# A hybrid decoder trunk: the attention's exponentials turned by VectorE and GpSimd transfers, and the mixers' small transfers taken off the weight queue

## The chip, the cores and the metric

The kernel runs on one core of one Trainium2 chip. The core has TensorE (PE), VectorE (DVE), ScalarE (ACT), GpSimd (POOL) and SyncE (SP); each takes its instructions in the order of the program. SP issues DMA transfers, and so can ACT and POOL. The metric is the device time of one execution in microseconds, as the median of several runs.

## The reference

Two layers of a decoder trunk for one sequence of 256 positions and a model width of 2048, all in float32:

```
for l in range(2):
    h = rms_norm(x, mix_norm[l])
    h = mixer_ab(h, ...) if l == 0 else mixer_c(h, ...)
    x = x + h
    x = x + conv_ffn(rms_norm(x, ffn_norm[l]), ...)     # gated, hidden width 5632
```

`mixer_ab` has one input projection whose parts go to two mixers: a chunked spatial gating (parts u and v) and HGRN2, a gated linear recurrence over 8 heads (q, f, i, g). `mixer_c` is attention with 16 heads of width 128, swept in blocks of 128 queries:

```
q, k, v, g, f = split(h @ w_in)
q = rms_norm(q per head, q_gain);  k = rms_norm(k per head, k_gain)
c = cumsum(log_sigmoid(f + b_f))                        # per head
s = q k^T * 128**-0.5 + c[query] - c[key]               # causal
o = softmax(s) @ v                                      # per head and query block
return (o * sigmoid(g)) @ w_out
```

For a head there are three blocks of 128 x 128 scores: queries 0-127 with keys 0-127, and queries 128-255 with keys 0-127 and 128-255.

## The kernel before, in words

**Weights.** All matrices are streamed once from HBM, 820 pieces of mostly 128 x 1024 values. SP's queue loads a piece into `w` (four buffers), ACT rounds it to `wh` (L175), DVE takes the rest `wl = w - wh` (L176), and PE multiplies in three parts: high by high, high by low, low by high (L292 to L294 in `project_tok`, L311 to L313 in `project_four`). One piece is 12 matmuls of 512 columns. `wh` and `wl` have three buffers here, so that ACT and DVE run some pieces ahead of PE.

**Turning a result.** `project_four` and `project_tok` leave tokens on the partitions, and most consumers want features there. So the result is evicted to `z`, DVE turns its 32 x 32 blocks into `tmp` (`blocks`, L324), and 16 small transfers of 32 KB put the blocks in place (`moves`, L331, rows of 256 bytes). Before the change these 16 alternate between SP's queue, where the weight loads are, and POOL's. This is done for f (`gates`), u (`spatial`), the gated HGRN output (`gated`), q and k of the attention, its gate (`gate`), and the results of both output projections (`add_four`), and for the FFN (`zt`), which the change leaves as it is.

**Order.** Side work is written as generators. `tick()` runs once ahead of each weight piece and takes every generator in flight to its next `yield`; `depth[0]` says how many may be in flight. A generator that has started transfers yields `LAG` = 6 times before it reads what they bring. `held` ties an instruction behind the latest `wh` or `wl`. The order on each engine is then set by the framework's scheduler, from these ties and from its own estimates; it is fixed when the kernel is built.

**Attention.** `mixer_c` handles four groups of four heads. For a group it projects q, k and v, and queues one generator `attend` per head, two in flight. In `attend`: ACT copies q and k with their gains (`qk`, L949); after one yield PE makes the scores (L954, L955), DVE adds the biases `ct` and `cb` and the causal mask and takes the maxima (L958 to L968), ACT takes the exponentials in place with their sums (`sc`, L98), DVE the reciprocals (L972). Two yields later PE turns the three blocks (L977) into PSUM, ACT copies them to `pt` (L980), and one yield later PE multiplies with v (L984 to L986) and ACT scales the result into `o` (L988). `cb` is spread over the partitions by a store to DRAM and four loads on POOL's queue (L928, L934). Then come the gate projections (`w_cg`), with `gate` waiting until all heads are done, and the output projections (`w_co`).

Of the kernel before, what the change touches and what calls it, by code (L numbers as in the profile page):

```python
# [15 lines left out]
P = 128  # L16
S = 256
# [8 lines left out]
LAG = 6  # L26
FORGET = 4
WAIT = 4
PACE = 4
# [24 lines left out]
def tile_trunk(ctx: ExitStack, tc: tile.TileContext, x, pp_d, cst_d, mlev_d, msk_d,  # L54
# [261 lines left out]

    def transposed(src, tmp, dst, queues=(nc.sync, nc.gpsimd)):

        blocks(src, tmp)
        moves(tmp, dst, queues)  # L320
# [5 lines left out]

    def moves(tmp, dst, queues=(nc.sync, nc.gpsimd), rows=range(4)):
        n = 2 * BLK
        for a in rows:
            for b in range(4):  # L330
                queues[(a + b) % len(queues)].dma_start(dst[BLK * b:BLK * (b + 1), :, a * n:(a + 1) * n],  # L331
                                  tmp[BLK * a:BLK * (a + 1), b * 4 * n:(b + 1) * 4 * n]
                                  .rearrange("p (m r) -> p m r", m=4))
# [125 lines left out]

    def add_four(q, ps, z, tmp, dst, nxt, halves=1):  # L460
        for T in range(2):
            SC.activation(z[:, T], ps[T], AF.Copy)
        blocks(lambda T: z[:, T], tmp)
        moves(tmp, dst, rows=range(4 // halves))

        def rest():
            if halves == 2:
                yield
                moves(tmp, dst, rows=range(2, 4))
            for _ in range(LAG - 2 * (q == 3)):  # L470
                yield
            for i in range(4):
                m = 4 * q + i
                held(V.tensor_tensor(xT[m], xT[m], dst[:, i], ALU.add), "wl")
                nxt.feed(m)
                if q < 3 or i % 2:
                    yield
            if q == 3:
                for _ in range(WAIT):
                    yield  # L480
                yield from nxt.finish_tok()

        queue.append(rest())


    def mixer_ab(norm):
# [281 lines left out]
        def gated(j):  # L768
# [42 lines left out]
        def spatial(j, z):  # L811
            for _ in range(LAG):
                yield
# [9 lines left out]
        for j in range(2):  # L823
# [4 lines left out]
            t = hp.tile([P, 1024], F32, tag="tok", name=nm("turn"), bufs=2)  # L828
            transposed(lambda T: z[:, T * 512:(T + 1) * 512], tmp, t.rearrange("p (m t) -> p m t", m=4))
            depth[0] = 4  # L830
# [14 lines left out]
        for q in range(4):  # L845
# [12 lines left out]
            if q == 0:  # L858
                depth[0] = 2
            add_four(q, ps, z, tmp, dst, nxt, 2 if q in (1, 2) else 1)  # L860
        es.close()
# [4 lines left out]
    def mixer_c(norm):  # L866
# [21 lines left out]
        R, Rt = norm.finish(), norm.Rt  # L888
        yB = []
        gq = hp.tile([P, LANE], F32, tag="gq", name="gq")[:, 0:1]  # L890
# [53 lines left out]

        def attend(h, q, k, v, o):
            d0 = (h % 4) * P
            qk = hp.tile([P, 2, S], F32, tag="qk", name=nm("qk"), bufs=2)
            for j, (t, g) in enumerate(((q, gq), (k, pp[:, C_KN:C_KN + 1]))):
                r = SC.activation(qk[:, j].rearrange("p (t n) -> p t n", t=2), turned(t[:, h % 4]), AF.Copy, scale=g)  # L949
                if j == 0:  # L950
                    held(r)
            yield
            sp = bank()
            PE.matmul(sp[:, 0:P], qk[:, 0, 0:P], qk[:, 1, 0:P], start=True, stop=True)  # L954
            PE.matmul(sp[:, P:3 * P], qk[:, 0, P:S], qk[:, 1], start=True, stop=True)  # L955
            sc = hp.tile([P, 3, P], F32, tag="sc", name=nm("sc"), bufs=3)
            scf = sc.rearrange("p a b -> p (a b)")
            V.scalar_tensor_tensor(scf[:, 0:P], sp[:, 0:P], ct[:, 0, h:h + 1], cb[:, h, 0:P],  # L958
                                   ALU.add, ALU.subtract)
            V.scalar_tensor_tensor(scf[:, P:3 * P], sp[:, P:3 * P], ct[:, 1, h:h + 1], cb[:, h],  # L960
                                   ALU.add, ALU.subtract)
            V.tensor_tensor(sc[:, 0::2], sc[:, 0::2], cst[:, K_CM:K_CM + P].unsqueeze(1)
                            .to_broadcast([P, 2, P]), ALU.add)
            mxs = hp.tile([P, LANE], F32, tag="mxs", name=nm("mxs"), bufs=2)[:, 0:2]
            sms = hp.tile([P, LANE], F32, tag="sms", name=nm("sms"), bufs=4)[:, 0:2]
            parts = ((0, P), (P, 3 * P))
            for T, (a, b) in enumerate(parts):
                V.tensor_reduce(mxs[:, T:T + 1], scf[:, a:b], AX.X, ALU.max, negate=True)  # L968
            for T, (a, b) in enumerate(parts):
                last = act(scf[:, a:b], scf[:, a:b], AF.Exp, bias=mxs[:, T:T + 1],  # L970
                           accum_out=sms[:, T:T + 1])
            V.reciprocal(sms, sms)  # L972
            yield
            yield
            pps = bank()
            for b in range(3):
                r = PE.transpose(pps[:, b * P:(b + 1) * P], sc[:, b], ident)  # L977
                tc.add_manual_dep(r.ins, last.ins.name, order, reason="in a row")
            pt = hp.tile([P, 3 * P], F32, tag="pt", name=nm("pt"), bufs=2)
            SC.activation(pt, pps[:, 0:3 * P], AF.Copy)  # L980
            yield
            op = bank()
            v0, v1 = (v[:, T, d0:d0 + P] for T in range(2))
            PE.matmul(op[:, 0:P], pt[:, 0:P], v0, start=True, stop=True)  # L984
            PE.matmul(op[:, P:S], pt[:, P:S], v0, start=True, stop=False)
            PE.matmul(op[:, P:S], pt[:, S:3 * P], v1, start=False, stop=True)  # L986
            for T in range(2):
                SC.activation(o[:, T, d0:d0 + P], op[:, T * P:(T + 1) * P], AF.Copy, scale=sms[:, T:T + 1])  # L988
            left[0] -= 1

# [9 lines left out]
        for g in range(CH // 4):  # L1000
            qkv = []
            ss = hp.tile([P, 2, 2, LANE // 4], F32, tag="ss", name=nm("ss"), bufs=2)[..., 0:4]
            for j in range(3):
# [12 lines left out]
                if j < 2:  # L1016
# [11 lines left out]
            os_.append(piece("o", CH // 4))  # L1028
            queue.extend(attend(h, *qkv, os_[g]) for h in range(4 * g, 4 * g + 4))

        room = []

        def gate(q, z):
# [7 lines left out]
            for _ in range(2 * (q < 2)):  # L1041
                yield
            moves(tmp, heads(t))
            for _ in range(LAG - 2 * (q == 3)):
                yield
            for i in range(4):
                if not room:
                    tag, n = ("big", 8) if not yB else ("o", 2)
# [4 lines left out]
                yB.append(y)  # L1053
                yield

        for q in range(CH // 4):
# [4 lines left out]
            queue.append(gate(q, z))  # L1061
        nxt = Norm(C_FFN + KT, turn=True)
        for q in range(4):
            ps = project_four(w_co[4 * q:4 * q + 4], yB, KT)
            add_four(q, ps, piece("z", 2), flat(piece("tmp", 2)), heads(piece("turn", 4)), nxt)
# [4 lines left out]
    def ffn(l, norm, last):  # L1070
# [69 lines left out]
        def add_y(q, finish):  # L1140
            tmp, zt = room()
            near = last and q == 2
            transposed(lambda T: y[:, T, q * 512:(q + 1) * 512], tmp, zt,
                       (nc.sync, nc.gpsimd, SC) if near else (nc.sync, nc.gpsimd))

# [155 lines left out]
```

## Time and profile before

| what | value |
|---|---|
| median of three runs | 2288.69 us (2287.63, 2288.69, 2288.85) |
| profiled execution, its span (the page gives no other time for it) | 2287.3 us |
| busy: PE, DVE, ACT, POOL | 2280.8, 1559.8, 1309.6, 361.2 us |
| granted TensorE clock (1.000 is full speed) | 1.000 |
| DMA | 480.45 MB, mean 210 GB/s; busy 5 to 8 tenths in each slice |

Stages by the span's clock: mixer A and B up to about 390 us, the first FFN to about 1100, the attention to about 1410, its gate and output projections to about 1585, the second FFN to the end. In the groups of the profile a line stands with its engine, operation and tiles, the busy time and the mean duration in ns, and then the idle time ahead of it with what ended that. A busy time is the union of the group's instructions; matmuls overlap, so a matmul's duration is not what it costs the stream. In the chain, SPq is the issuing side of SP's queue.

### The profile page before, as it was taken

To read this page: it belongs to the slowest core of one execution; us is meant where nothing else is said; L and a number is where in the kernel's file an instruction comes from. 1 tells how busy PE (TensorE), PEld (TensorE's weight loads), DVE (VectorE), ACT (ScalarE), POOL (GpSimd) and SP (SyncE) were. 2 spreads that over 40 slices of the span, in tenths; PEclk is the share of its full clock that TensorE was granted. 3 is DMA by queue.
4 is the path that set the end of the run, shared out by engine and by line. 5 is a ranking of instruction groups with operands and counts; after the bars stand their busy time and mean duration, and the time that the engine had idled before them with its cause. 6 is when DMAs were issued, how large, how long until landed. Compare 5 with 4: busy or idle time off the path is not lost.

```text
span 2287.3 us, 32261 instructions
## 1 busy us (share of the span) xinstructions
PE 2280.8 (100%) x10832; PEld 1893.5 (83%) x10832; DVE 1559.8 (68%) x2309; ACT 1309.6 (57%) x1980; POOL 361.2 (16%) x662
## 2 busy tenths in 40 slices
PE   9999999999999999999999999999999999999999
PEld 8888888888888888888888888888888888888887
DVE  7788767777467656766875675767776476657766
ACT  7677756666456445654565555655665465456642
POOL 0121221212012002111111111211211012012102
PEclk9999999999999999999999999999999999999999
DMA  8655767778667667776666655777777677667765
GB/s 288 195 169 160 215 199 235 238 216 234 193 208 221 206 201 213 220 213 186 213 227 203 194 177 181 220 224 242 225 217 218 195 216 210 209 205 216 223 204 174
DMA packets 489415, 480.45 MB, mean 210 GB/s; under 512 B 114112, under 2 KB 457168, under 8 KB 489120
## 3 DMA queue, kind: packets, MB, share of 16 engines
q1 hardware_dynamic: 467040, 453.54, 64.2%
q0 software_dynamic: 20480, 22.50, 4.3%
q10 hardware_dynamic: 1728, 2.35, 0.3%
q8 instruction: 85, 1.39, 0.3%
q14 instruction: 82, 0.67, 0.1%
HBM read 435.24 MB, written 2.11 MB: 191 GB/s over the span
## 4 chain that ended last, share of the span: by engine, by line
PE 97%; DVE 2%; ACT 1%; issue 0%; SPq 0%; DMA 0%; DVEq 0%; ACTq 0%
PE pm L311 26%; PE pm L312 26%; PE pm L313 26%; PE pm L292 4%; PE pm L294 4%; PE pm L293 4%; PE pm L193 1%; PE pm L266 1%; PE pm L217 1%; DVE wl L176 0%; PE pm L269 0%; ACT wh L175 0%; DVE kq L701 0%; PE px L955 0%; SPq L331 0%
## 5 line engine op out<-in xcount | busy, mean ns | idle before, releaser
L176 DVE TENSOR_TENSOR wl<-w,wh 128x1024 fp32r<-128x1024 f32 (+1 forms) x820 | 996.9, 1219 | 637.0 <-ACT wh L175 629.3
L175 ACT ACTIVATE wh<-w 128x1024 fp32r<-128x1024 f32 (+1 forms) x820 | 862.5, 1054 | 786.0 <-PE pm L313 552.3
L311 PE MATMUL pm<-wh,a 128*128 128x512 f32 x1728 | 674.4, 390 | 0.0
L312 PE MATMUL pm<-wl,a 128*128 128x512 f32 x1728 | 672.5, 389 | 0.0
L313 PE MATMUL pm<-wh,a 128*128 128x512 f32 x1728 | 672.5, 389 | 0.0
L331 POOL DMA_DIRECT2D zt<-tmp x413 | 223.5, 549 | 1201.6 <-DVE tmp L324 1089.8
L313 PEld LDWEIGHTS pm<-wh,a 128*128 128x128 f32 x1728 | 324.4, 188 | 67.4
L312 PEld LDWEIGHTS pm<-wl,a 128*128 128x128 f32 x1728 | 324.4, 188 | 67.3 <-DVE wl L176 0.5
L311 PEld LDWEIGHTS pm<-wh,a 128*128 128x128 f32 x1728 | 324.4, 188 | 67.1
L311 PE MATMUL pm<-wh,hid 128*128 128x512 f32 x688 | 267.6, 389 | 0.0
L312 PE MATMUL pm<-wl,hid 128*128 128x512 f32 x688 | 267.6, 389 | 0.0
L313 PE MATMUL pm<-wh,hid 128*128 128x512 f32 x688 | 267.6, 389 | 0.0
L331 POOL DMA_DIRECT2D turn<-tmp x160 | 86.7, 550 | 504.5 <-DVE tmp L324 256.7
L292 PE MATMUL pm<-wh,a 128*128 128x512 f32 x416 | 165.2, 397 | 0.0
L294 PE MATMUL pm<-wh,a 128*128 128x512 f32 x416 | 162.1, 390 | 0.0
L293 PE MATMUL pm<-wl,a 128*128 128x512 f32 x416 | 162.0, 389 | 0.0
L311 PEld LDWEIGHTS pm<-wh,hid 128*128 128x128 f32 x688 | 129.2, 188 | 26.9
L313 PEld LDWEIGHTS pm<-wh,hid 128*128 128x128 f32 x688 | 129.2, 188 | 26.8
L312 PEld LDWEIGHTS pm<-wl,hid 128*128 128x128 f32 x688 | 129.2, 188 | 26.7
L1105 ACT ACTIVATE conv<-zt,pp 128x256 f32<-128x256 f32 x176 | 95.9, 589 | 26.1 <-DMA zt<-tmp 22.2
L324 DVE STREAM_TRANSPOSE tmp<-z 128x512 f32<-128x512 f32 x120 | 83.4, 704 | 18.9 <-ACT z L1091 18.4
L294 PEld LDWEIGHTS pm<-wh,a 128*128 128x128 f32 x416 | 78.1, 188 | 16.6
(244 smaller groups left out, 2075.6 us busy)
## 6 DMA issues: line engine op xcount, KB each, us to landing
w<-in_w_up SPq DMA_DIRECT2D x352, 512.0 KB, 4.4
w<-in_w_dn SPq DMA_DIRECT2D x176, 512.0 KB, 4.5
w<-in_w_cqkv SPq DMA_DIRECT2D x96, 512.0 KB, 4.3
w<-in_w_abo SPq DMA_DIRECT2D x32, 512.0 KB, 4.6
w<-in_w_cg SPq DMA_DIRECT2D x32, 512.0 KB, 4.3
w<-in_w_co SPq DMA_DIRECT2D x32, 512.0 KB, 4.3
zt<-tmp SPq DMA_DIRECT2D x414, 32.0 KB, 2.7
zt<-tmp POOLq DMA_DIRECT2D x413, 32.0 KB, 2.5
```

The source lines that it names most:

```text
L175: r = deep["wh"] = SC.activation(wh, w, AF.Copy)
L176: deep["wl"] = V.tensor_tensor(wl, w, wh.bitcast(F32), ALU.subtract)
L193: PE.matmul(ps[g][T], a[:, o + T * P:o + (T + 1) * P], t[:, i * 512:(i + 1) * 512], start=k + i + j == 0, stop=k + i == KT - 1 and j == 2)
L292: PE.matmul(ps[T], ah, h, start=k + i == 0, stop=False)
L293: PE.matmul(ps[T], ah, l, start=False, stop=False)
L294: deep["last"] = PE.matmul(ps[T], al, h, start=False, stop=k + i == KT - 1)
L311: PE.matmul(ps[T], ah, h, start=not begun and k + i == ks[0], stop=False)
L312: PE.matmul(ps[T], ah, l, start=False, stop=False)
L313: deep["mm"] = deep["last"] = PE.matmul(ps[T], al, h, start=False, stop=not more and k + i == ks[-1] + 1)
L324: V.transpose(tmp.rearrange("p (b m i t) -> p b m i t", b=4, m=4, t=2)[:, :, :, :, T], src(T).rearrange("p (m b j) -> p b m j", m=4, b=4))
L331: queues[(a + b) % len(queues)].dma_start(dst[BLK * b:BLK * (b + 1), :, a * n:(a + 1) * n], tmp[BLK * a:BLK * (a + 1), b * 4 * n:(b + 1) * ...
L1105: held(SC.activation(c, z, AF.Identity, bias=pp[:, cb:cb + 1], scale=w(2)))
```

## The change

In the attention PE no longer turns the exponentials. `attend` takes two heads, their scores share one buffer of six blocks; DVE turns the 32 x 32 blocks of the exponentials into `ptmp`, and 16 transfers on POOL's queue, in rows of 128 bytes, build `pt` for both heads. The value matmuls follow `LAG - 1` yields after the last transfers. A pair starts at least `PAIR` = 5 ticks after the one before it.

All small transfers of the mixers go on POOL's queue alone, except where `q` is 3 in `gate` and `add_four`. Those that read them wait one more yield. The two halves of `add_four` for the second and third results are gone. The depth is 3 while the gate is projected, and `yB` is filled by index.

```
+PAIR = 5
+    ONE, TWO = (nc.gpsimd,), (nc.sync, nc.gpsimd)
-    def moves(tmp, dst, queues=(nc.sync, nc.gpsimd), rows=range(4)):
+    def moves(tmp, dst, queues=TWO):
...
-    def add_four(q, ps, z, tmp, dst, nxt, halves=1):
+    def add_four(q, ps, z, tmp, dst, nxt):
...
-        moves(tmp, dst, rows=range(4 // halves))
+        moves(tmp, dst, ONE if q < 3 else TWO)
         def rest():
-            if halves == 2:
-                yield
-                moves(tmp, dst, rows=range(2, 4))
-            for _ in range(LAG - 2 * (q == 3)):
+            for _ in range(LAG + 1 - 3 * (q == 3)):
                 yield
...
         def gates(j, z):
-            for _ in range(LAG):
+            for _ in range(LAG + 1):
...
-            transposed(lambda T: z[:, T * 512:(T + 1) * 512], tmp, t.rearrange("p (m t) -> p m t", m=4))
+            transposed(lambda T: z[:, T * 512:(T + 1) * 512], tmp, t.rearrange("p (m t) -> p m t", m=4), ONE)
...
-            moves(tmp, t.rearrange("p (m t) -> p m t", m=4))
-            for _ in range(LAG - 1):
+            moves(tmp, t.rearrange("p (m t) -> p m t", m=4), ONE)
+            for _ in range(LAG):
...
-        def attend(h, q, k, v, o):
+        turn = [0]
+        def attend(hs, q, k, v, o):
+            while steps[0] < turn[0]:
+                yield
+            turn[0] = steps[0] + PAIR
...
-            sc = hp.tile([P, 3, P], F32, tag="sc", name=nm("sc"), bufs=3)
+            sc = hp.tile([P, 6, P], F32, tag="sc", name=nm("sc"), bufs=1)
...
             yield
             yield
-            pps = bank()
-            for b in range(3):
-                r = PE.transpose(pps[:, b * P:(b + 1) * P], sc[:, b], ident)
-                tc.add_manual_dep(r.ins, last.ins.name, order, reason="in a row")
-            pt = hp.tile([P, 3 * P], F32, tag="pt", name=nm("pt"), bufs=2)
-            SC.activation(pt, pps[:, 0:3 * P], AF.Copy)
-            yield
+            tmp = hp.tile([P, 6 * P], F32, tag="ptmp", name=nm("ptmp"), bufs=1)
+            for i, sms in enumerate(sums):
+                V.reciprocal(sms, sms)
+                t = V.transpose(tmp.rearrange("p (b m i) -> p b m i", b=4, m=6)[:, :, 3 * i:3 * i + 3],
+                                sc[:, 3 * i:3 * i + 3].rearrange("p m (b j) -> p b m j", b=4))
+                if i == 0:
+                    held(t, "wl")
+            yield
+            n = 6 * BLK
+            pt = hp.tile([P, 6, P], F32, tag="pt", name=nm("pt"), bufs=2)
+            for a in range(4):
+                for b in range(4):
+                    nc.gpsimd.dma_start(pt[BLK * b:BLK * (b + 1), :, BLK * a:BLK * (a + 1)],
+                                        tmp[BLK * a:BLK * (a + 1), b * n:(b + 1) * n]
+                                        .rearrange("p (m r) -> p m r", m=6))
+                if a == 1:
+                    yield
+            for _ in range(LAG - 1):
+                yield
...
-                    transposed(lambda T: z[:, T], flat(piece("tmp", 2)), heads(t))
+                    transposed(lambda T: z[:, T], flat(piece("tmp", 2)), heads(t), ONE)
...
-            moves(tmp, heads(t))
-            for _ in range(LAG - 2 * (q == 3)):
+            moves(tmp, heads(t), ONE if q < 3 else TWO)
+            for _ in range(LAG + 1 - 3 * (q == 3)):
```

`spatial` changes as `gates` does.

More of the change, by code (lines that the diff above doesn't have):

```diff
@@ L315, in project_four, with transposed @@
         return ps
-    def transposed(src, tmp, dst, queues=(nc.sync, nc.gpsimd)):
+    ONE, TWO = (nc.gpsimd,), (nc.sync, nc.gpsimd)
+    def transposed(src, tmp, dst, queues=TWO):
         blocks(src, tmp)
@@ L811, in spatial @@
         def spatial(j, z):
-            for _ in range(LAG):
+            for _ in range(LAG + 1):
                 yield
@@ L859, in mixer_ab @@
                 depth[0] = 2
-            add_four(q, ps, z, tmp, dst, nxt, 2 if q in (1, 2) else 1)
+            add_four(q, ps, z, tmp, dst, nxt)
         es.close()
@@ L960, in attend @@
[L960 to L972, printed above, removed]
+            sps = []
+            for qk in qks:
+                sp = bank()
+                PE.matmul(sp[:, 0:P], qk[:, 0, 0:P], qk[:, 1, 0:P], start=True, stop=True)
+                PE.matmul(sp[:, P:3 * P], qk[:, 0, P:S], qk[:, 1], start=True, stop=True)
+                sps.append(sp)
@@ new lines, in attend @@
+            sums = []
+            for i, (h, sp) in enumerate(zip(hs, sps)):
+                c0 = 3 * P * i
+                parts = ((c0, c0 + P), (c0 + P, c0 + 3 * P))
+                V.scalar_tensor_tensor(scf[:, c0:c0 + P], sp[:, 0:P], ct[:, 0, h:h + 1], cb[:, h, 0:P],
+                                       ALU.add, ALU.subtract)
+                V.scalar_tensor_tensor(scf[:, c0 + P:c0 + 3 * P], sp[:, P:3 * P], ct[:, 1, h:h + 1], cb[:, h],
+                                       ALU.add, ALU.subtract)
+                V.tensor_tensor(sc[:, 3 * i:3 * i + 3:2], sc[:, 3 * i:3 * i + 3:2],
+                                cst[:, K_CM:K_CM + P].unsqueeze(1).to_broadcast([P, 2, P]), ALU.add)
+                mxs = hp.tile([P, LANE], F32, tag="mxs", name=nm("mxs"), bufs=2)[:, 0:2]
+                sms = hp.tile([P, LANE], F32, tag="sms", name=nm("sms"), bufs=4)[:, 0:2]
+                for T, (a, b) in enumerate(parts):
+                    V.tensor_reduce(mxs[:, T:T + 1], scf[:, a:b], AX.X, ALU.max, negate=True)
+                for T, (a, b) in enumerate(parts):
+                    act(scf[:, a:b], scf[:, a:b], AF.Exp, bias=mxs[:, T:T + 1], accum_out=sms[:, T:T + 1])
+                sums.append(sms)
@@ new lines, in attend @@
+            yield
+            n = 6 * BLK
+            pt = hp.tile([P, 6, P], F32, tag="pt", name=nm("pt"), bufs=2)
+            for a in range(4):
+                for b in range(4):
[4 more added lines that the diff above has]
+                    yield
@@ new lines, in attend @@
+            for _ in range(LAG - 1):
+                yield
+            for i, (h, sms) in enumerate(zip(hs, sums)):
+                d0 = (h % 4) * P
+                op = bank()
+                v0, v1 = (v[:, T, d0:d0 + P] for T in range(2))
+                p0, p1, p2 = (pt[:, 3 * i + m] for m in range(3))
+                PE.matmul(op[:, 0:P], p0, v0, start=True, stop=True)
+                PE.matmul(op[:, P:S], p1, v0, start=True, stop=False)
+                PE.matmul(op[:, P:S], p2, v1, start=False, stop=True)
+                for T in range(2):
+                    SC.activation(o[:, T, d0:d0 + P], op[:, T * P:(T + 1) * P], AF.Copy, scale=sms[:, T:T + 1])
+                left[0] -= 1
@@ L1028, in mixer_c @@
             os_.append(piece("o", CH // 4))
-            queue.extend(attend(h, *qkv, os_[g]) for h in range(4 * g, 4 * g + 4))
+            queue.extend(attend((h, h + 1), *qkv, os_[g]) for h in range(4 * g, 4 * g + 4, 2))
         room = []
+        depth[0] = 3
         def gate(q, z):
```

39 lines of the change are left out of this document (14 added, 25 removed).

## The prediction

> **What bounds the kernel now.** I read the page first: its engine line, then its chain of waits.
>
> ```profile
> span 2287.3 us, 32261 instructions
> PE 2280.8 (100%) x10832; PEld 1893.5 (83%) x10832; DVE 1559.8 (68%) x2309; ACT 1309.6 (57%) x1980; POOL 361.2 (16%) x662
> ...
> PE 97%; DVE 2%; ACT 1%; issue 0%; SPq 0%; DMA 0%; DVEq 0%; ACTq 0%
> ```
>
> TensorE (PE) fills the span, and 97% of the chain that ended last lies on it. So the time can only fall by what leaves PE's stream or by what PE waits for, and it rises only if something makes PE wait. Next come the waits that PE itself had, all of them:
>
> ```profile
> PE px L681 <- ACT o L753: 1.1, 1, 1.1
> PE warm L144 <- DVE ones L84: 1.1, 1, 1.1
> PE pm L312 <- DVE wl L176: 0.6, 1, 0.6
> ```
>
> That is 2.8 us in 2287. Anything gained beyond 3 us must be PE work that disappears.
>
> **Term 1: the transposes leave PE.** Line 977 turns the exponentials on PE, three 128x128 blocks a head. The change deletes these 48; in the order of the changed program every other PE instruction is still there, so "it removes nothing" is no rival. The price is read in the PE timeline at one of the eight places (columns: start, duration, engine, line, operation):
>
> ```profile
> 1391.72 0.39 PE L311 MATMUL pm<-wh,a 128*128 128x512 f32 x1
> ...
> 1392.40 0.39 PE L311 MATMUL pm<-wh,a 128*128 128x512 f32 x1
> 1392.62 0.39 PE L312 MATMUL pm<-wl,a 128*128 128x512 f32 x1
> 1392.85 0.39 PE L313 MATMUL pm<-wh,a 128*128 128x512 f32 x1
> 1393.08 0.82 PE L977 MATMUL px<-cst,sc 128*128 128x128 f32 x6
> 1393.65 0.47 PE L311 MATMUL pm<-wh,a 128*128 128x512 f32 x1
> 1393.97 0.39 PE L312 MATMUL pm<-wl,a 128*128 128x512 f32 x1
> ```
>
> A 512-column matmul starts every 0.227 us (1391.72 to 1392.40 is three of them); its 0.39 us is a latency that overlaps the next. Without the six transposes the L311 would start at 1393.08 and the L312 at 1393.31 instead of 1393.97: 0.66 us for six. The chain in order of time charges the same; these are the first and last of its eight entries:
>
> ```profile
> 1177.00 0.66 PE px L977 x6
> ...
> 1410.24 0.66 PE px L977 x6
> ```
>
> 8 x 0.66 = **5.3 us** gained. The bounds: nothing is added to PE, so not below 0; and at most the time in which any transpose was in flight, 6.5 us:
>
> ```profile
> L977 PE MATMUL px<-cst,sc 128*128 128x128 f32 x48 | 6.5, 272 | 0.0
> ```
>
> Here a rule can be weighed. The Trainium skill (TensorE: Matmul & The Clock Gate, Part 4: PE-mode transpose) gives a 128x128 transpose about 275 ns within a kernel. The trace agrees on the duration (272), but the starts lie 0.11 us apart, since six cost 0.66. Charged by duration, 48 would be worth 13 us; that is the last rival.
>
> **Term 2: a weight load that stood behind transfers.** The chain leaves PE at one place for SP's queue:
>
> ```profile
> 338.54 1.95 SPq L331
> 343.81 4.01 DMA w<-in_w_abo
> 347.91 1.07 ACT wh L175
> 349.00 1.24 DVE wl L176
> ```
>
> SP's timeline shows it, and ACT's shows a second place:
>
> ```profile
> 337.24 6.47 SPq L331 DMA_DIRECT2D dst<-tmp  x8
> 343.81 8.29 SPq L181 DMA_DIRECT2D w<-in_w_abo  x6
> ```
>
> ```profile
> 1420.48 1.06 ACT L175 ACTIVATE wh<-w 128x1024 fp32r<-128x1024 f32 x1 [1.66 <-PE pm L313]
> 1426.33 1.06 ACT L175 ACTIVATE wh<-w 128x1024 fp32r<-128x1024 f32 x1 [4.79 <-DMA w<-in_w_cg]
> ```
>
> Eight small transfers hold SP for 6.47 us ahead of the weight load; that ended in PE's 0.6 us wait on wl (row above). At 1426 ACT waited 4.79 us for a weight without a wait of PE; its usual wait is 1.66, for PE to free a buffer, so PE's splits run about 3 us ahead (4.79 - 1.66). The change moves 23 batches of eight transfers, 184, from SP to GpSimd (POOL): gates, gated and spatial two each, q and k eight, gate three, add_four six. These two places are among them: **0.6 us** gained. Bounds 0 and 1.7 (with the 1.1 us at L681, in whose neighbourhood ACT and DVE are reordered); I take 0.6, the wait whose cause is the queue.
>
> **Term 3: POOL takes over.** It gets the 184 and another 128 for the exponentials (8 pairs of heads x 16). POOL's group, and the landing of both queues' transfers:
>
> ```profile
> L331 POOL DMA_DIRECT2D turn<-tmp x160 | 86.7, 550 | 504.5 <-DVE tmp L324 256.7 <-issue 82.9 <-ACT wh L175 62.0
> DMA to landing us min/median/max: 1.7/2.0/6.3
> ```
>
> Sixteen on one queue take 16 x 0.55 = 8.8 us instead of 4.4 beside SP's, so a turned tile lands 4.4 us later. The consumers move too: in the changed order ACT's first read of the k tile stands three weight chunks later than before, of f and u two; a chunk is 12 matmuls, 12 x 0.227 = 2.72 us, so 5.4 to 8.2 us later against 4.4. Where q is 3 in gate and add_four both queues and the old distance (four steps) stay. Cost 0 on PE; if a tile were late, ACT or VectorE (DVE) would block in order, and behind it the weight splits wh and wl that PE needs.
>
> The pair's own path: score matmuls at t; in the changed PE order the value matmuls follow nine chunks and eight small matmuls (four of its own scores, four of the next pair's) later, t + 9 x 2.72 + 0.9 = t + 25.4. DVE's work for one pair, as it stands now:
>
> ```profile
> 1404.13 0.35 DVE L958 SCALAR_TENSOR_TENSOR sc<-px,ct,cb 128x128 f32<-128x128 f32 x1 [1.06 <-PE px L955]
> ...
> 1409.84 0.16 DVE L972 RECIPROCAL sms<-sms 128x2 f32<-128x2 f32 x1
> ```
>
> The scores of that pair start on PE about 0.85 us ahead of 1404.13, so the last reciprocal is at t + 6.7 with two weight splits in between. Two block transposes of 384 columns follow (L324 in term 4: 0.70 us for 512, so 0.53 each) and one more split at most: tile ready at t + 9. Then 8.8 us of issue and 2.0 of landing: t + 19.8, 5.6 us ahead of need. The longest landing (6.3) leaves 1.3.
>
> The trace has no transfer in 128-byte rows. The nearest rows are the 256-byte ones, 550 ns. The count of rows a transfer goes from 128 to 192; in proportion that is 0.82 us and t + 24.1, still ahead. PE starts to wait at (25.4 - 9 - 2.0)/16 = 0.90 us apiece. I take 0.55: issue is 0.51 us for 16 rows and 0.55 for 128, so the count hardly shows:
>
> ```profile
> 1156.47 0.51 POOL L928 DMA_DIRECT2D cd<-fc  x1
> 1158.44 2.18 POOL L934 DMA_DIRECT2D cb<-cd  x4 [1.46 <-DMA cd<-fc]
> ...
> 1278.56 3.78 POOL L331 DMA_DIRECT2D turn<-tmp  x7 [2.52 <-issue]
> ```
>
> The last row is a pause of 2.52 us that POOL takes now and then; inside a batch it leaves 3 of the 5.6 us. In a group of four heads POOL then issues 64 transfers, 35 us in 24 chunks of 2.72: half its time.
>
> The first two rows carry one more cost. The cd and cb loads queue behind the k tile's 16 transfers, so 4.4 us later. The landing of cb, and DVE's first use of it:
>
> ```profile
> DMA to landing us min/median/max: 9.1/11.1/14.1
> ```
>
> ```profile
> 1170.89 0.35 DVE L958 SCALAR_TENSOR_TENSOR sc<-px,ct,cb 128x128 f32<-128x128 f32 x1 [0.63 <-PE px L955]
> ```
>
> The first of four lands at 1158.4 + 9.1 + 4.4 = 1171.9, DVE wants it at 1170.9: a wait of 1 us with a wl split queued behind it, within the 3 us that the splits are ahead, so 0; with the longest landing (5 us later) it costs up to 2 us, once.
>
> **Term 4: ACT and DVE.** ACT loses 16 copies (L980), DVE gains 16 block transposes:
>
> ```profile
> L980 ACT ACTIVATE pt<-px 128x384 f32<-128x384 f32 x16 | 6.8, 480 | 0.0
> L324 DVE STREAM_TRANSPOSE tmp<-z 128x512 f32<-128x512 f32 x120 | 83.4, 704 | 18.9 <-ACT z L1091 18.4 <-ACT z L462 0.4
> ```
>
> ```profile
> 140.00:190.00 50.00, 48.82 (x518) 41.23 (x517) 44.05 (x114) 35.84 (x112) 12.16 (x18) 1.00 0.54 159
> 1300.00:1400.00 100.00, 100.00 (x476) 83.83 (x475) 61.30 (x94) 57.90 (x103) 11.56 (x22) 1.00 0.63 194
> ```
>
> 16 x 0.53 = 8.5 us on a DVE that is 61% busy in the attention (last row: window, length, then PE, PEld, DVE, ACT): hidden. The tight place is the HGRN stage (DVE 44.05 of 50, where PE loses 1.2 us). The change adds no work there, only another order: 0, bounded by about a repeat of these 1.2 us either way.
>
> **Sum.** 5.3 + 0.6 = 5.9 us. The profiled span is 2287.3 us; the three runs are 0.3 to 1.6 above it, their median 1.4. 2288.69 - 5.9 = **2282.8 us**. About 0.2%, 4.6 us here, is what a measurement of this kernel can tell from no change, so the forecast clears that line (2284.1) by 1.3 us.
>
> **Rivals.** *Cover runs thin.* The waits of terms 2 to 4 come back in small pieces: the cb wait (up to 2), the HGRN order (1.2), no gain at 349 (0.6), one late tile. For it: the splits run 3 us ahead, no more. Against: reads were moved by more than the transfers. Price 2 to 5 us, so 2285 to 2288, no measurable change.
>
> *POOL becomes the bound* (slower). If a 128-byte-row transfer holds POOL for c us, each pair's value matmuls wait 16c - 14.4 us, eight times. From c = 0.98 this eats the 5.9 and another 4.6; at twice the row, 1.10, it is 8 x 3.2 = 26 us: 2308. For it: rows of this size are not in the trace. Against: POOL's 548/548/665 ns (least, median, longest), beside a DVE that is 61% busy in the attention:
>
> ```profile
> L331 POOL DMA_DIRECT2D turn<-tmp x160: 548/548/665, 74.3 to 1570.6; - x160
> ```
>
> The Trainium skill (SBUF — State Buffer, SBUF: two separate sides) speaks for this rival: GpSimd cannot write DMA descriptors while VectorE runs a two-port operation, so such transfers belong on the SP or ACT queue; its example is 620 ns alone and 3100 beside one. In that ratio c would be 2.75 and the time about 2520, an estimate from that page. The row just shown disagrees for this kernel's operations, block transposes among them: none of 160 took over 665 ns.
>
> *Transposes cost PE their duration.* 48 x 0.272 = 13.1, so 2288.7 - 13.1 - 0.6 = 2275; the start times speak against it.
>
> **How the numbers follow.** Forecast 0.62, thin cover 0.22, POOL bound 0.14, full duration 0.02. Faster 0.64, same 0.22, slower 0.14. The range runs from 2280 (6.5 + 1.7 gained, 2280.5) up through the thin-cover cases to 2291, which leaves out POOL's heavy prices and 2275; the forecast's own range is 2281 to 2284.
>
> **What would show it.** Right: no PE transposes, PE still 100% with about 5 us less busy time, no L312 wait near 349, pt transfers at 0.55 us on POOL, PE never waiting for pt. Wrong: value matmuls waiting on a DMA, wl or wh waiting for POOL-fed tiles, pt transfers of 0.9 us or more.

## The result and the profile after

| kernel | median | kernel before on the same chip | difference | ratio (95% interval) |
|---|---|---|---|---|
| changed | 2284.64 us (21 runs) | 2287.66 | -3.0 us | 0.9987 (0.9981 to 0.9993) |
| changed, second chip | 2285.34 us (11 runs) | 2287.89 | -2.6 us | 0.9990 (0.9981 to 0.9998) |
| changed, third chip | 2284.09 us (11 runs) | 2287.74 | -3.7 us | 0.9987 (0.9977 to 0.9996) |

The change gains about 3 us, 0.13%. The forecast was 5.9 us. By the prediction's own line of 0.2% this is no change that a few runs could tell; it takes these many runs to see it. The profiled execution has a span of 2282.8 us at 2284.62 us.

The page of the changed kernel, its engine line and its chain:

```profile
span 2282.8 us, 32108 instructions
PE 2275.3 (100%) x10784; PEld 1889.1 (83%) x10784; DVE 1565.0 (69%) x2325; ACT 1303.8 (57%) x1964; POOL 530.4 (23%) x974
...
PE 95%; DVE 2%; issue 1%; ACT 1%; DMA 1%; POOL 0%; DVEq 0%; ACTq 0%; POOLq 0%
```

PE has 48 instructions and 5.5 us of work less (2280.8 before). Its share of the chain went from 97% to 95%, but that is not time that PE lost: its waits add up to 3.8 us, against 2.8 before. These are all of them (us in total, times, longest):

```profile
PE px L681 <- ACT o L753: 1.6, 2, 1.3
PE pm L313 <- DVE wl L177: 1.1, 2, 0.9
PE warm L145 <- DVE ones L85: 1.1, 1, 1.1
```

The wait on wl near 349 has gone. There are two others on wl, the longer of 0.9 us, and the wait in the HGRN stage has grown from 1.1 to 1.6. No value matmul waits for `pt`. The new transfers on POOL, and their landing:

```profile
L1000 POOL DMA_DIRECT2D pt<-ptmp x128: 565/565/597, 1179.6 to 1416.4; - x128
DMA to landing us min/median/max: 1.7/4.1/5.9
```

A transfer in 128-byte rows holds POOL for 0.565 us (least and median; 0.597 at most).

To see where time comes from, the starts of the same PE matmul in two traces can be set against each other: there are 9912 such matmuls with weights, in the same order in every kernel here. The table gives what each stage gained against the profiled execution of before, in us (worked out from the traces; minus is a loss). The kernels of the lower rows are described below.

| kernel | HGRN, 150 to 230 | 345 to 360 | 375 to 400 | 1000 to 1030 | attention, 1172 to 1440 | 1440 to 1530 |
|---|---|---|---|---|---|---|
| changed | -0.44 | +0.92 | -0.49 | -1.27 | +5.67 | 0.00 |
| changed, second profile | -0.43 | +0.92 | -1.01 | -1.19 | +5.67 | -1.41 |
| changed, third profile | -0.42 | +0.92 | 0.00 | -1.13 | +5.67 | 0.00 |
| no turning (e3) | +1.08 | +0.39 | 0.00 | 0.00 | +5.67 | 0.00 |
| attention half (e1) | -0.16 | +0.87 | 0.00 | 0.00 | +4.45 | 0.00 |
| attention half, again | +1.12 | +0.92 | 0.00 | 0.00 | +4.35 | 0.00 |
| queue half (e2) | -0.45 | +0.92 | 0.00 | -1.05 | +0.17 | -0.44 |
| queue half, ten more transfers (e5) | -0.44 | +0.92 | 0.00 | 0.00 | -1.04 | -0.97 |
| first mixer's queues (e10) | -0.42 | +0.92 | 0.00 | -1.15 | +0.17 | 0.00 |
| attention mixer's queues (e6) | +0.34 | +0.51 | 0.00 | 0.00 | +0.17 | -0.21 |
| changed, ten more transfers (e4) | -0.42 | +0.92 | -0.45 | 0.00 | +5.05 | 0.00 |
| assembled (e9) | -0.15 | +0.39 | 0.00 | 0.00 | +4.13 | -1.70 |

The attention column holds the first term: 5.67 us in all three profiles. What is taken back stands in the other columns, and the largest and steadiest piece, 1.1 to 1.3 us, is at 1012 us, in the FFN, which the change does not touch.

Most rows add up to more than the measured gain, because the profiled execution of before was a long one. Its span is 2287.3 us; on the three other chips of the experiments the kernel before has median spans of 2286.6, 2286.0 and 2285.9 us, and 6 of its 89 executions there reach 2287.3. So part of what the rows show as gained is a wait that this one execution of before had and others of its kind do not have.

### The profile page after: what moved, and what is told of

Read it like the earlier page. It is cut to its first block, busy times and chain, and to the rows that moved or that the text cites. A ratio compares the mean times of both kernels' runs of the same rounds, so it can differ in the third digit from the quotient of the medians.

```text
span 2282.8 us, 32108 instructions
## 1 busy us (share of the span) xinstructions
PE 2275.3 (100%) x10784; PEld 1889.1 (83%) x10784; DVE 1565.0 (69%) x2325; ACT 1303.8 (57%) x1964; POOL 530.4 (23%) x974
## 4 chain that ended last, share of the span: by engine, by line
PE 95%; DVE 2%; issue 1%; ACT 1%; DMA 1%; POOL 0%; DVEq 0%; ACTq 0%; POOLq 0%
PE pm L312 26%; PE pm L313 26%; PE pm L314 26%; PE pm L293 4%; PE pm L294 4%; PE pm L295 4%; PE pm L194 1%; PE pm L267 1%; DVE wl L177 1%; PE pm L270 1%; DMA dst<-tmp 1%; PE pm L218 1%; ACT wh L176 0%; DVE st L732 0%; DVE kq L701 0%
## 5 line engine op out<-in xcount | busy, mean ns | idle before, releaser
L334 POOL DMA_DIRECT2D turn<-tmp x304 | 164.9, 550 | 268.4 <-DVE tmp L327 136.8
```

## The experiments

The theory (A) was that the transposes are worth their 5.3 us and that the other half of the change gives part of it back. The rival (B) was that the transposes are worth only about 3 us and the rest is neutral.

### The two halves, and no turning at all

**e1, the attention half.** Before, with only the new `attend` (and its depth and index):

```
-            queue.extend(attend(h, *qkv, os_[g]) for h in range(4 * g, 4 * g + 4))
+            queue.extend(attend((h, h + 1), *qkv, os_[g]) for h in range(4 * g, 4 * g + 4, 2))
```

> The attention half of the change alone: pairs of heads, exponentials turned by VectorE blocks and 16 GpSimd transfers a pair; every other small transfer stays on both queues as before. Theory A (the transposes are worth their 5.3 us; the other half of the change gives part of it back): 5.3 us under the kernel before, 2282.4 where before is at 2287.7; the GpSimd pause stays in the feed-forward batch at about 909, where it cost nothing, and there is no wait of TensorE near 1012. Theory B (the transposes are worth only about 3 us, the rest of the change is neutral): 2284.7, as the whole change. If a pair's turned exponentials come late, TensorE waits at the value matmuls and the gain is smaller than 5.3 by these waits.

Measured: 2283.88 us beside 2288.47, -4.6 us, ratio 0.9982 (0.9973 to 0.9990). No wait near 1012, as expected. Of the 5.67 us in the attention, 1.2 are missing (4.45 in the table); that comes back below.

**e2, the queue half.** The changed kernel with the old `attend` and its depth:

```
-            queue.extend(attend((h, h + 1), *qkv, os_[g]) for h in range(4 * g, 4 * g + 4, 2))
+            queue.extend(attend(h, *qkv, os_[g]) for h in range(4 * g, 4 * g + 4))
```

> The queue half of the change alone: small transfers of the mixers on GpSimd's queue and the later reads, with the exponentials turned on TensorE as before. Theory A: this half costs what the whole change lacks, 5.3 - 3.0 = 2.3 us: 2290.0 where before is at 2287.7. In the trace: no wait of TensorE near 349 (0.6 to 0.9 us gained), but one near 386 (0.4 us), some 0.5 us more in the HGRN stage and 1.2 us near 1012, where the GpSimd pause falls into the last batch ahead of the down projection. Theory B: neutral, 2287.7 within 0.5. The forecast's own term: 0.6 faster, 2287.1.

Measured: 2291.16 us, +2.7 us, ratio 1.0012 (1.0004 to 1.0021). So the queue half alone makes the kernel slower. Its trace has no wait near 349, 0.45 us lost in the HGRN stage and 1.05 us at 1012, all as theory A has it; the wait near 386 did not come in this execution.

**e3, no turning.** Before without L977 and L980:

```
-                r = PE.transpose(pps[:, b * P:(b + 1) * P], sc[:, b], ident)
...
-            SC.activation(pt, pps[:, 0:3 * P], AF.Copy)
+            pt = scf
```

> The kernel before without any turning of the exponentials (48 transposes and 16 copies left out; the value matmuls read the exponentials unturned, so this part of the computation is missing). Theory A: 48 transposes cost 5.3 us of TensorE: 2282.4 where before is at 2287.7, with eight steps of 0.66 us in TensorE's timeline. Theory B: about 3 us, 2284.7. Charged by their duration of 272 ns: 13 us, 2275.

Measured: 2282.79 us, -5.7 us, ratio 0.9976 (0.9965 to 0.9986). The matmuls that stood around the six transposes at 1393.08 in the prediction now follow each other every 0.227 us:

```profile
1387.60 0.39 PE L313 MATMUL pm<-wh,a 128*128 128x512 f32 x1
1387.82 0.39 PE L311 MATMUL pm<-wh,a 128*128 128x512 f32 x1
1388.05 0.39 PE L312 MATMUL pm<-wl,a 128*128 128x512 f32 x1
```

The attention column reads 5.67, the same as in the changed kernel. Of this, 0.17 us is not the transposes': e2, e6 and e10 below keep them and gain 0.17 there too. This settles the first term: 48 transposes cost PE 5.5 us, and DVE's block transposes and POOL's transfers take all of that away at no cost to PE within the attention. Rival B is out.

### What stands at 1012 us

POOL, ACT, DVE and PE of the changed kernel there (start, duration, engine, line; in brackets the idle time before and what ended it):

```profile
991.54 2.71 POOL L334 DMA_DIRECT2D zt<-tmp  x5 [17.43 <-DVE tmp L327]
996.48 1.63 POOL L334 DMA_DIRECT2D zt<-tmp  x3 [2.23 <-issue]
...
1003.19 1.09 ACT L1135 ACTIVATE conv<-zt,pp 128x256 f32<-128x256 f32 x2 [4.16 <-DMA zt<-tmp]
...
1003.82 0.97 DVE L1136 SCALAR_TENSOR_TENSOR conv<-zt,pp,conv 128x255 f32<-128x255 f32 x2 [3.54 <-ACT conv L1135]
...
1012.69 0.50 PE L313 MATMUL pm<-wl,hid 128*128 128x512 f32 x1 [0.94 <-DVE wl L177]
```

and the same batch before:

```profile
991.87 4.33 POOL L331 DMA_DIRECT2D zt<-tmp  x8 [17.43 <-DVE tmp L324]
...
999.27 1.08 ACT L1105 ACTIVATE conv<-zt,pp 128x256 f32<-128x256 f32 x2
```

POOL issues five of eight transfers, pauses 2.23 us, and issues the other three. ACT's convolution then starts at 1003.19 instead of 999.27 and has waited 4.16 us for the landing; DVE is held up, the weight splits behind it are late, and PE waits. The delay is longer than the pause. This is the landing of the three late transfers, and of POOL's eight before:

```profile
DMA to landing us min/median/max: 3.0/3.9/5.1
```

```profile
DMA to landing us min/median/max: 1.9/2.7/3.5
```

SP sends its next two weight loads at 996.49 and 997.07, among the late three (996.48, 997.02 and 997.56), and the last of these lands at 1002.65. Before, POOL's last transfer is out at 995.65, ahead of the first weight load at 996.88. That the weight loads slow the late transfers is read from this order; no run tried it alone.

The pause is the one that the prediction saw once, at 1278.56. Counting POOL's transfers from 0 shows its rule in these traces: the 113th and 219th come after a pause in all fourteen, and the 325th in the eight that reach it ahead of the attention, whenever that is. The count holds on through the attention if a transfer of `pt` (192 rows) is taken as one and a half of the others (128 rows): the pauses that show (1.5 to 2.8 us, ended by nothing the profile knows) are then 105 to 110 apart, or two or three times that. Before, the 113th and 219th are at 494.4 and 908.8 us, in the FFN, and neither costs PE anything. The change gives POOL 72 transfers more by then (the first mixer's and those of its addition), so the 325th falls into the batch at 991, the last ahead of the down projection, whose tile is read at once.

**e4, ten transfers more.** They move the pause ten places up without touching the FFN:

```
+            if j == 0:
+                for i in range(10):
+                    nc.gpsimd.dma_start(pads[i][:, :, 0:64], tmp[0:BLK, 0:4 * 64].rearrange("p (m r) -> p m r", m=4))
             queue.append(gates(j, t))
```

> The changed kernel with ten more GpSimd transfers of the same form (32 rows of four 256-byte pieces, to DRAM, read by nobody) behind the first gate batch at about 85 us. Theory A: the GpSimd pause comes at a fixed count of transfers, so it moves ten places up, out of the last batch of the feed-forward network at 991 into the batch at 970, the wait near 1012 goes: 1.2 us under the changed kernel, 2283.4 where that is at 2284.6. Rival: the pause isn't what TensorE waits for near 1012 (a weight load or the order of VectorE's work): the time stays within 0.3 us of the changed kernel and the wait stays.

Measured: 2284.24 us beside 2288.47, -4.2 us, ratio 0.9982 (0.9973 to 0.9991), so 0.6 to 1.7 us better against before than the three comparisons of the changed kernel. The times alone do not settle it (the intervals reach 2 us to either side); the trace does. PE, ACT and DVE run the same instructions in the same order as in the changed kernel, and POOL's pause has moved:

```profile
970.12 1.63 POOL L336 DMA_DIRECT2D zt<-tmp  x3 [17.43 <-DVE tmp L329]
974.12 2.71 POOL L336 DMA_DIRECT2D zt<-tmp  x5 [2.37 <-issue]
993.52 4.33 POOL L336 DMA_DIRECT2D zt<-tmp  x8 [16.70 <-DVE tmp L329]
```

The pause is in the batch at 970, the batch at 993 runs through, and the loss at 1012 is 0.00. Theory A holds. It comes with a new loss of 0.6 us in the attention, where the scores once wait for `qk`: a later pause, of 2.69 us, now stands inside the batch of a k tile, at 1377.

**The changed kernel again**, twice, on other chips:

> The changed kernel once more, unchanged, to have it beside the others on one chip and a second profile of it. Theory A (the wait near 1012 belongs to the place of the GpSimd pause and so comes in every execution; the wait near 349 of the kernel before was of one execution): 3.0 to 4.0 us under the kernel before, again a wait of TensorE of about 1 us near 1012. If the waits are accidents of one execution, the one near 1012 is gone.

> The changed kernel beside the attention half and the assembled version. Theory A: 3 us under the kernel before, and the wait near 1012 a third time, since the pause comes at the same count of transfers. Rival: no wait there.

Measured: -2.6 and -3.7 us (table above). Both profiles have the pause at the same transfer and lose 1.19 and 1.13 us at 1012. With e2, e10 and the twice-issued kernel below, six traces of six in which the 325th transfer is in that batch lose 1.05 to 1.27 us there; all others lose nothing.

**e5, the queue half with ten transfers more:** e2 with the lines of e4.

> The queue half of the change alone with the ten more GpSimd transfers behind the first gate batch, so that the GpSimd pause leaves the batch at 991. Theory A: 1.1 us under the queue half without them, so about 1.6 us over the kernel before (2.7 - 1.1), and no wait near 1012. Rival (the pause is a small part, the queue half loses in the mixers): within 0.4 us of the queue half, 2.3 to 3.1 over before.

Measured: 2290.57 us beside 2287.89, +2.7 us, ratio 1.0011 (1.0002 to 1.0020). A miss: the loss at 1012 is gone, but the time is no better than e2's. The trace says why. A later pause moved as well, into a gate batch:

```profile
1462.33 1.63 POOL L336 DMA_DIRECT2D turn<-tmp  x3 [11.74 <-ACT yc L381]
1466.33 5.95 POOL L336 DMA_DIRECT2D turn<-tmp  x11 [2.36 <-issue]
...
1477.93 1.22 ACT L381 ACTIVATE yc<-turn 128x256 fp32r<-128x256 f32 x2 [1.19 <-DMA turn<-tmp]
```

That costs 0.97 us near 1480. Another 1.2 us is lost at 1177, where DVE takes `cb` 3 us later than before (1173.97 instead of 1170.89) and PE's transposes wait behind the exponentials.

### Where the queue half loses

**e6, the attention mixer's q, k and gates alone** on POOL's queue, the rest as before (against the kernel before):

```
-                    transposed(lambda T: z[:, T], flat(piece("tmp", 2)), heads(t))
+                    transposed(lambda T: z[:, T], flat(piece("tmp", 2)), heads(t), ONE)
...
-            moves(tmp, heads(t))
-            for _ in range(LAG - 2 * (q == 3)):
+            moves(tmp, heads(t), ONE if q < 3 else TWO)
+            for _ in range(LAG + 1 - 3 * (q == 3)):
```

> Of the queue half only the attention mixer's q, k and gate transfers on GpSimd's queue (its later reads with them); the first mixer and both additions of a mixer's output as before, exponentials on TensorE as before. Theory A (the queue half loses in the first mixer: its one-queue batches, the order of the HGRN stage, and the pause that they move): no change, within 0.5 us of the kernel before. Rival (the loss is in the attention mixer, where q and k come later): 1 to 2.7 us over it.

Measured: 2288.78 us beside 2287.89, +0.9 us, ratio 1.0004 (0.9995 to 1.0013): between the two expectations, and not told from no change.

**e10, the first mixer and both additions alone:** e2 with the lines of e6 taken back.

> Of the queue half only the first mixer's transfers and the two additions of a mixer's output on GpSimd's queue, with the later reads; the attention mixer's q, k and gates and its exponentials as before. Theory A (the loss lies here: HGRN order 0.45 us, the pause in the batch at 991 1.1 us, landing waits of the one-queue additions up to 0.5): 1.5 to 2 us over the kernel before, with waits near 386 and 1012 in TensorE's timeline. Rival (the loss lies in the attention mixer): within 0.5 us of it.

Measured: 2289.36 us beside 2287.74, +1.6 us, ratio 1.0008 (0.9999 to 1.0017), as expected by theory A, with 0.42 us lost in the HGRN stage and 1.15 us at 1012; the wait near 386 did not come. The two parts add to 2.5 us, and e2 measured 2.7.

In e2 the loss near 1480 is the pause, 2.50 us inside the gate batch at 1472, as in e5. In the changed kernel the losses near 386 and 1480 come in some executions only. Its second profile has both. This is its gate batch:

```profile
1458.56 7.02 POOL L334 DMA_DIRECT2D turn<-tmp  x13 [13.83 <-ACT yc L379]
1465.85 1.09 POOL L334 DMA_DIRECT2D turn<-tmp  x2 [0.27 <-DMA turn<-tmp]
1469.12 0.55 POOL L334 DMA_DIRECT2D turn<-tmp  x1 [2.19 <-DMA turn<-tmp]
...
1473.51 1.21 ACT L379 ACTIVATE yc<-turn 128x256 fp32r<-128x256 f32 x2 [1.59 <-DMA turn<-tmp]
```

POOL's transfers take eight semaphores in turn in this program, so in a batch of 16 on one queue each of the last eight waits until the one eight places before it has landed. Here the last waits 2.19 us for the eighth, which landed at 1468.84; the tile is late by 1.59 us for ACT, and PE loses 1.4 us near 1480. In the first profile the same batch waits 0.73 us and PE loses nothing. Near 386 it is a batch of the first mixer's addition, for which DVE waits:

```profile
377.71 0.76 DVE L474 TENSOR_TENSOR x<-x,dst 128x256 f32<-128x256 f32 x2 [3.91 <-DMA dst<-tmp]
```

PE loses 1.0 us behind it. In the first profile DVE waits 3.35 us there and PE loses 0.5, in the third 2.59 and nothing.

### POOL made to work twice

**e7.** Each of the 128 transfers of the exponentials is issued twice.

```
                     nc.gpsimd.dma_start(pt[BLK * b:BLK * (b + 1), :, BLK * a:BLK * (a + 1)],
...
+                    nc.gpsimd.dma_start(twins.pop()[:, :, 0:BLK],
+                                        tmp[BLK * a:BLK * (a + 1), b * n:(b + 1) * n]
...
```

> The changed kernel with each of the 128 transfers of the exponentials issued twice (the second copy goes to DRAM and is read by nobody), so 32 instead of 16 a pair. By the prediction's term 3 with what the changed kernel's trace shows (tile ready 7.3 to 8.7 us after the scores, 16 transfers issued in 9.6 to 10.6, need at 27.2): the last is issued at about t+28.5 and lands 2.3 later, so TensorE waits about 4 us at each of eight places: some 30 us over the changed kernel, 2310 to 2320. Rival (the GpSimd issue isn't on the path, a transfer costs less when it is one of many): under 2290.

Measured: 2298.79 us (2 runs) beside 2287.89, ratio 1.0046 (1.0028 to 1.0064), 13.5 us over the changed kernel on that chip: less than half of the 30 expected, and more than the rival's. PE waits for `pt` at five places instead of eight:

```profile
PE px L1017 <- issue: 5.4, 3, 3.7
PE px L1017 <- DMA pt<-ptmp: 4.1, 2, 3.2
```

The expectation held the order of PE's work fixed. The scheduler moved it: the value matmuls of the second pairs now start 50 to 57 us behind their scores instead of 27.2, and three of the four find `pt` ready. So this run shows that late transfers do make PE wait, but it does not price a single transfer's threshold.

### A version put together, and the attention half again

**e9.** The new `attend`, q and k on POOL's queue, all else on both queues; against e1:

```
-                    transposed(lambda T: z[:, T], flat(piece("tmp", 2)), heads(t))
+                    transposed(lambda T: z[:, T], flat(piece("tmp", 2)), heads(t), ONE)
```

> A version put together from the runs so far: the attention half of the change, and of the queue half only q and k on GpSimd's queue; gates, the first mixer and the additions stay on both queues as before. Theory A (the queue half loses in the first mixer, in the gate batches and by the pause that it moves; the wait behind SP's small transfers, here 0.8 us near 1310 in the attention half alone, goes with q and k): 5 us under the kernel before, 2 under the changed kernel, and as fast as the attention half alone or up to 0.8 us faster. Rival (the queue half is worth having and only accidents made it slow): no faster than the changed kernel.

**The attention half** beside it:

> The attention half alone once more, unchanged, beside the changed kernel on one chip and for a second profile. Theory A: 4.5 us under the kernel before and 1.5 to 2 under the changed kernel; the wait near 1310 belongs to one execution (a weight load behind SP's eight small transfers) and may come at another place. Theory B (the whole change is worth as much as the attention half): within 0.5 us of the changed kernel.

Measured on one chip, before at 2287.74: e9 2286.68 us, -1.1 us, ratio 0.9997 (0.9988 to 1.0006); the attention half 2283.65 us, -4.1 us, 0.9984 (0.9975 to 0.9992); the changed kernel 2284.09 us, -3.7 us.

The assembled version is a clear miss. The wait that it was to remove is gone, but the pause fell into two bad places. At its 326th transfer, in the first batch of `pt`, and in the addition of a result to x:

```profile
1177.94 0.60 POOL L1003 DMA_DIRECT2D pt<-ptmp  x1 [9.59 <-DVE ptmp L994]
1181.04 5.04 POOL L1003 DMA_DIRECT2D pt<-ptmp  x9 [2.50 <-issue]
```

```profile
1193.66 0.58 DVE L994 STREAM_TRANSPOSE ptmp<-sc 128x384 f32<-128x384 f32 x1 [4.21 <-DMA pt<-ptmp]
1194.16 1.18 DVE L177 TENSOR_TENSOR wl<-w,wh 128x1024 fp32r<-128x1024 f32 x1
```

```profile
1500.76 2.17 POOL L334 DMA_DIRECT2D turn<-tmp  x4 [2.04 <-issue]
...
1509.52 0.52 ACT L355 ACTIVATE a<-x,pp 128x256 fp32r<-128x256 f32 x1 [5.61 <-DVE x L477]
```

`ptmp` has one buffer, so DVE must wait 4.21 us for the delayed transfers to read it, with a weight split queued behind: 1.5 us on PE. The other costs 1.7 us near 1512.

The attention half loses 1.2 and 1.3 us near 1310 in its two profiles, so this is no accident of one execution, as I had put it. It is POOL's pause again, and not a weight load behind SP's small transfers:

```profile
1293.61 2.17 POOL L332 DMA_DIRECT2D turn<-tmp  x4 [17.07 <-DVE tmp L325]
1297.47 2.17 POOL L332 DMA_DIRECT2D turn<-tmp  x4 [1.69 <-issue]
```

```profile
1298.28 12.81 SPq L182 DMA_DIRECT2D w<-in_w_cqkv  x7
```

```profile
1304.56 0.94 ACT L957 ACTIVATE qk<-turn,pp 128x256 f32<-128x256 f32 x2 [4.27 <-DMA w<-in_w_cqkv]
```

The last row names a weight load, but `qk` reads the turned k tile and no weights. POOL pauses 1.69 us in the middle of that tile's batch (1.68 in the other profile, ahead of the same transfer, the 401st). Its last two transfers go out behind SP's first weight load, at 1298.55 and 1299.09, and land at 1302.61 and 1304.25, 4.1 and 5.2 us after their issue; the one at 1298.01 took 1.8. ACT starts 0.3 us after the last landing. Before, without a pause in this batch, POOL's eight land in 1.8 to 2.2 us. As at 1012, the pause costs more than its length.

On one chip the attention half and the changed kernel are 0.4 us apart, within what these runs can tell. No version measured here is shown to beat the changed kernel.

## Why the prediction was right or wrong

**Term 1** was right in kind and in size: 5.3 us forecast, 5.5 measured (the 5.67 of four traces with the transposes gone, less the 0.17 that kernels with the transposes gain there as well). The price read from starts (0.11 us each) and not from durations (0.272 us) is the right one; 13 us would have shown.

**Term 2** had the right mechanism, and its size came from one execution. The profile of before lost 0.92 us near 349. Five other traces with the same queues there (e1, e1 again, e3, e6, e9) gain 0.87, 0.92, 0.39, 0.51 and 0.39 against it, so with the 0.92 of before the loss is 0.4 us on average. I put 0.6. The second place that I named, at 1426, is not quite "without a wait of PE" either: the late `wl` ends at 1428.65, its matmul starts at 1428.71, and PE loses 0.15 us there, in this trace and no other. It is most of the 0.17.

**Term 3, POOL's issue and its cost of 0 on PE,** is where the forecast failed, though not in the attention. The arithmetic for a pair held. I had the tile ready at t + 9, the last issue at t + 17.8 and the need at t + 25.4; the changed kernel's trace shows t + 7.3 to 8.7, t + 17.8 to 19.6 and t + 27.2. 0.55 us was right for a 128-byte-row transfer (0.565), so POOL did not become the bound. The Trainium skill (SBUF — State Buffer, SBUF: two separate sides) has POOL held up while VectorE runs a two-port operation; with 597 ns for the longest transfer above, no such hold-up shows beside the operations of this kernel. The `cb` wait came, 0.40 us, and was hidden, as forecast:

```profile
1173.91 0.35 DVE L973 SCALAR_TENSOR_TENSOR sc<-px,ct,cb 128x128 f32<-128x128 f32 x1 [0.40 <-DMA cb<-cd]
```

What I mis-sized is the pause. I called it something that POOL takes now and then, and weighed it only inside a batch of `pt`, at its own length. It comes at a fixed count of transfers, so more transfers early move every later pause, and the transfers behind it can land later still. This one cost 1.1 to 1.3 us in a stage that the change does not touch. The landing waits within batches of 16 on one queue were not in the sum either: 0.5 us on average near 386 and 0.5 near 1480, over the three profiles of the changed kernel.

**Term 4.** The order of the HGRN stage was put at 0 with a bound of 1.2 us. In all eight traces with the new order of the first mixer PE loses 0.42 to 0.45 us against the profile of before. With the old order the six traces give 0, -0.16, +1.12, +1.08, +0.34 and -0.15, 0.4 us on average. The difference is 0.8 us. These kernels change the first mixer's queues as well as its order; the chain through this stage (PE behind ACT's `o`, behind DVE) has no transfer in it, so I put the 0.8 down to the order, but no run tried the order alone.

**The sum**, with the measured sizes: 5.5 + 0.4 - 0.8 - 1.2 - 0.5 - 0.5 = 2.9 us, and the three comparisons gave 3.0, 2.6 and 3.7. The size is thus accounted for. The single steps are shown in the traces; for the averages of the waits that come and go, a handful of executions is all there is.

The likeliest case lost to the rival *cover runs thin*, which had 0.22 and named the HGRN order and a small gain at 349, but not the pause. The chance of 0.64 for a gain over 0.2% was too high: the forecast cleared that line by 1.3 us, and four costs that I had set at 0 (the pause, the HGRN order, and the landing waits at two places) took 3.0 us together. In absolute time the forecast looks nearer than it was: 2282.8 started from 2288.69, the median of three runs, and 21 runs put the kernel before at 2287.66. That 1.0 us is luck.

## What to carry to other kernels

Charge a PE instruction by the distance of starts around it; that number held to 0.2 us over 48 of them. Where a software queue is given more transfers, look for what it does at a fixed count: the price can land in a stage that was not edited, it can be larger than the pause when weight loads go out meanwhile, and a version built by adding the good parts can lose to each of them. Do not book the removal of a wait at the size it has in one profile; five traces with the same queues show that 349 is not always 0.9.

## What the runs showed of the hardware

POOL's pause: 2.1 to 2.8 us ahead of the 113th and 219th of these 32 KB transfers (counted from 0), and of the 325th where it comes ahead of the attention; the 113th pauses in kernels that reach it at 333 and at 494 us alike. Why it comes was not tried.

In e7, a wait of 3.16 us halved the clock that PE was granted. PE's rows behind that wait, and two stretches of the trace (window, length, PE, PEld, DVE, ACT, POOL, clock, DMA share, GB/s):

```profile
1202.41 0.77 PE L1017 MATMUL px<-v,pt 128*128 128x128 f32 x2 [3.16 <-DMA pt<-ptmp]
...
1206.39 0.63 PE L295 MATMUL pm<-wh,a 128*128 128x512 f32 x1
1206.82 0.63 PE L296 MATMUL pm<-wl,a 128*128 128x512 f32 x1
1207.24 0.63 PE L297 MATMUL pm<-wh,a 128*128 128x512 f32 x1
```

```profile
1196.00:1200.00 4.00, 3.25 (x15) 2.36 (x13) 3.86 (x10) 1.80 (x4) 3.24 (x6) 1.00 0.78 195
1204.00:1208.00 4.00, 4.00 (x14) 3.42 (x13) 1.21 (x2) 1.34 (x5) 4.00 (x8) 0.50 0.51 135
```

At 0.50 the matmuls start 0.43 us apart instead of 0.227, for 5.5 us (1202.4 to 1207.9 in the timeline): this wait costs PE nearly twice its length. The other long wait of this run, 3.66 us up to 1285.35, also halves the clock, but only from about 1286.5 to 1290, when PE is at work again; it costs about one and a half times its length. The waits of about 1 us in the other traces leave the clock at 1.00. The Trainium skill (TensorE: Matmul & The Clock Gate, Part 1: The HAM clock gate) has the clock halve after an idle window of about 3.4 us; the trace agrees in kind, with 3.16 us of idle being enough here. So a price per wait that is linear in its length, as my rivals had it, is too low for waits as long as these two.
